# A decoder layer on one core: 8-word and 4-word runs behind the heads, the last output units, and the gate's transpositions inside two other blocks of a head

## The chip, the cores and the metric

The kernel runs on one core of a Trainium2 chip. Its engines are named as the profile names them: PE (TensorE matmul), PEld (its weight loads), DVE (VectorE), ACT (ScalarE), POOL (GpSimd) and SP (SyncE, which only issues transfers here). The metric is the time of one execution in device microseconds; of several runs the median counts.

## The reference

The reference is a decoder trunk of depth one: attention, the residual, and a final norm. All is float32, with 256 positions and a width of 4096.

```python
proj = rms_norm(x, norm_attn) @ w_in            # 256 x 4096  @  4096 x 16384 -> q | k | v | gate
z = q @ k.T / sqrt(128)                         # per head, 32 heads of 128, strictly causal
log_fail = where(causal, log_sigmoid(-z), 0)
suffix = cumsum(log_fail, reverse=True) - log_fail
a = where(causal, exp(log_sigmoid(z) + suffix), 0)
o = a @ v                                       # stick-breaking attention
h = x + (o * silu(gate)) @ w_out                # 4096 x 4096
out = rms_norm(h, final_norm)
```

## The kernel before, in words

**Products.** Every float32 operand of the two large multiplications is split into a high and a low fp32r part (`wh`, `wl` of the weights, which stream through PE; `sh`, `sl` of the input's rows and `oh`, `ol` of the gated heads, which are PE's stationary operands). One product of 128 x 128 by 128 x 512 is a triple of matmuls into one accumulator: high by high, high by low, low by high (`mm3`, called by `product`). A triple's matmuls visit their 512 columns in runs of 8 words ("e") or of 4 words ("c"): in the program's order these read `128x4x16x8` and `128x4x32x4`. The results are the same. Which form a matmul has is set by `BEHIND_OTHERS` for the first seven triples behind any other PE work (three letters, one for each matmul of a triple), by `IN_STEP` for the first triple of a step, and is "e" elsewhere. The counter `since_others` starts again with each block of other work, which comes through `ten`.

**Units and steps.** The work is 20 units one behind the other, each in 16 steps over the 4096 rows of the weights. Units 0 to 15 multiply `w_in`, each giving q, k, v and gate of two heads. Units 16 to 19 multiply `w_out`, each giving two blocks of 512 output columns for both halves of the rows. Units 0 and 16 are plain, with 8 triples a step. In the others a step is done in 8 triples ("eight") or, Strassen-like, in 7 ("seven"). A seven-step costs DVE three extra sums of weight tiles (`raw<-raw,raw` and `raw<-raw` in the profile) and POOL an accumulating transfer. The lists `SEVEN` (input units) and `SEVEN_OUT` (output units) say which steps are sevens. Unit 19, the last, takes its steps in the order `LAST_STEPS`, and three of its steps of `SEVEN_OUT` (11, 13, 14) are done as eights.

**Heads.** The two heads of an input unit are worked between the triples of the next unit, as blocks of PE work with ACT and DVE between them: four transpositions of q and k (`tr`), the scores (`z`), the scan of the sums along a row (`scan`: four matmuls into `z`), the transposition of the gate's two tiles (`gated_with`, its own block), and values (`out_of_head`). A ring named "att" holds a single PSUM bank for all these, one block at a time. The gate is made by `gate`: ACT and DVE turn it into its SiLU in place, in `gv_sb`.

**The planner.** Class `Plan` runs the whole program once as a simulation of the engines with costs in nanoseconds, and writes each engine's instructions in the order in which the simulation starts them. Rings (`take` and `give`) stand for buffers, and a work item carries a key: the smaller key goes first on its engine. So a change of a key, a cost or a ring changes the order of many later instructions. On the chip each engine runs its instructions in that order.

**The end.** While an output unit runs, the blocks of the unit before it are finished: DVE adds the residual (`h<-h,xres`), ACT sums the squares (`sq<-h`), DVE multiplies by the final gain (`gain_on`, `h<-h,grow`). Behind the last unit `last_h`, `block_done`, `part_done`, `finish` and `rows_out` finish the last two blocks, make the factor of each row and multiply and store all rows. Rows 128 to 255 are done ahead of rows 0 to 127; names such as `h6_1` are the block and the half of the rows. Keys and the cost of `squares` decide which of these small instructions go first.

Of the kernel before, what the change touches and what calls it, by code (L numbers as in the profile page):

```python
# [19 lines left out]
P = 128  # L20
S = 256
# [15 lines left out]
BEHIND_OTHERS = ("ccc", "ecc", "eee", "cce", "eee", "eee", "ecc")  # L37
# [9 lines left out]
SEVEN_OUT = (1, 2, 4, 5, 7, 10, 11, 13, 14)  # L47
# [17 lines left out]
H_LATER = 6  # L65
ON_SCALAR = ((1, 3, 5), (1, 3))
# [45 lines left out]
class Plan:  # L112
# [72 lines left out]
    def take(self, *names):  # L185
# [12 lines left out]

        return request
# [48 lines left out]
def kernel(  # L248
# [546 lines left out]
    def gate(u):  # L795
# [3 lines left out]
        yield nc.take("gh")  # L799
# [23 lines left out]
    def head(u, i):  # L823
        yield nc.take("att", "gh")
# [14 lines left out]
        yield nc.take("att")  # L839
        z = att.tile([P, BW], F32, tag="att", name=f"z{u}_{i}")  # L840
# [10 lines left out]
        yield nc.take("gh")  # L851
# [13 lines left out]
        yield nc.take("gh", "gh")  # L865
# [14 lines left out]
        yield nc.take("gh")  # L880
# [11 lines left out]
        o = st["both", u, i][:, 1, :]  # L892
# [11 lines left out]
        gated = st["gated", u, i]  # L904
# [3 lines left out]
    def gated_with(u, i):  # L908
        yield nc.until(("gate", u))
        yield nc.take("att")  # L910
        both = st["both", u, i] = att.tile([P, 2, S], F32, tag="att", name=f"o{u}_{i}")
        gT = both[:, 0, :]

        def turn():
            for t in range(NT):
                nc.tensor.transpose(gT[:, t * P : (t + 1) * P], st["gv", u][:, t, i * P : (i + 1) * P], ident)

        yield ten(turn, P, P)
        if i == 0:
            yield nc.take("gh")  # L920
            st["o", u] = wp.tile([P, 4, P], F32, tag="gh", name=f"gated{u}", bufs=ROWS)
        gated = st["gated", u, i] = st["o", u][:, 2 * i : 2 * i + 2, :].rearrange("p a b -> p (a b)")
        yield act(lambda: nc.scalar.copy(gated, gT), S)
        nc.tell(("gated", u, i))
# [113 lines left out]
    def squares(c, t, place, cut, key=None):  # L1038
# [6 lines left out]
            cut.stop - cut.start, key and key - 1e3,  # L1045
# [9 lines left out]
    def block_out(c, t, key):  # L1055
# [10 lines left out]
        yield from gain_on(c, t, key)  # L1066
# [270 lines left out]
```

## Time and profile before

| what | value |
|---|---|
| three runs | 1705.84, 1709.23 and 1709.48 us, median 1709.23 |
| the profiled execution's own time | 1706.34 us |
| its span, from first to last instruction | 1704.6 us |
| PE busy | 1685.6 us (99%), 7776 matmuls |
| DVE busy | 1607.4 us (94%) |
| ACT busy | 1202.5 us (71%) |
| POOL busy | 325.0 us (19%) |

The profiled execution is 2.9 us below the median of the three runs, which lie in two places 3.4 us apart. Matmuls overlap by design in the profile's model: one that is shown as 0.39 us long is followed by the next after 0.22 us, so the distance between starts is what to read, not the duration. Times on the axis count from the start of the span. All lines of the kernel are shown as L131, a helper through which every instruction goes; so the groups are told apart by the names of their tiles.

### The profile page before, as it was taken

To read this page: it belongs to the slowest core of one execution; us is meant where nothing else is said; L and a number is where in the kernel's file an instruction comes from. 1 tells how busy PE (TensorE), PEld (TensorE's weight loads), DVE (VectorE), ACT (ScalarE), POOL (GpSimd) and SP (SyncE) were. 2 spreads that over 40 slices of the span, in tenths; PEclk is the share of its full clock that TensorE was granted. 3 is DMA by queue.
4 is the path that set the end of the run, shared out by engine and by line. 5 is a ranking of instruction groups with operands and counts; after the bars stand their busy time and mean duration, and the time that the engine had idled before them with its cause. 6 is when DMAs were issued, how large, how long until landed. Compare 5 with 4: busy or idle time off the path is not lost.

```text
span 1704.6 us, 25109 instructions
## 1 busy us (share of the span) xinstructions
PE 1685.6 (99%) x7776; PEld 1415.9 (83%) x7776; DVE 1607.4 (94%) x2025; ACT 1202.5 (71%) x1633; POOL 325.0 (19%) x400
## 2 busy tenths in 40 slices
PE   9999999999999999999999999999999999999996
PEld 7888888888888888888888888888888888888785
DVE  8889999999999999999999999999999977999997
ACT  8986767676767676767676768686767765666664
POOL 0012222222222222221212121212122112122110
PEclk9999999999999999999999999999999999999998
DMA  9968887979797878797978797878788977889795
GB/s 348 329 197 246 231 245 220 255 212 256 208 269 196 269 197 272 195 279 195 268 204 261 208 256 213 254 216 248 220 243 224 295 244 241 240 251 284 218 293 187
DMA packets 248439, 412.78 MB, mean 242 GB/s; under 512 B 28016, under 2 KB 72560, under 8 KB 248304
## 3 DMA queue, kind: packets, MB, share of 16 engines
q1 hardware_dynamic: 194544, 354.24, 62.2%
q0 software_dynamic: 53472, 56.65, 20.5%
q8 instruction: 61, 1.00, 0.2%
q14 instruction: 74, 0.61, 0.1%
q10 hardware_dynamic: 288, 0.28, 0.0%
HBM read 402.93 MB, written 8.13 MB: 241 GB/s over the span
## 4 chain that ended last, share of the span: by engine, by line
PE 94%; DVE 3%; issue 1%; DMA 1%; ACT 0%; SPq 0%; DVEq 0%; ACTq 0%
PE acc L131 90%; PE z L131 2%; PE o L131 2%; DVE wl L131 1%; PE tr L131 1%; DVE h L131 0%; DVE raw L131 0%; ACT wh L131 0%; DMA raw<-in_w_in_dram 0%; DMA raw<-in_w_out_dram 0%; DMA xres<-in_x_dram 0%; DVE wh L131 0%; DVE gv_sb L131 0%; SPq L131 0%; DVE scalars L131 0%
## 5 line engine op out<-in xcount | busy, mean ns | idle before, releaser
L131 ACT CAST wh<-raw 128x1024 fp32r<-128x1024 f32 (+1 forms) x989 | 918.2, 969 | 370.8 <-DVE raw L131 166.8
L131 DVE TENSOR_TENSOR wl<-raw,wh 128x1024 fp32r<-128x1024 f32 (+1 forms) x815 | 974.9, 1219 | 56.4 <-ACT wh L131 25.1
L131 PE MATMUL acc<-wh,sh 128*128 128x512 f32 x2048 | 774.3, 390 | 0.3 <-DVE sh L131 0.3
L131 PE MATMUL acc<-wh,sl 128*128 128x512 f32 x1898 | 727.9, 383 | 1.2 <-DVE sl L131 1.2
L131 PE MATMUL acc<-wl,sh 128*128 128x512 f32 x1748 | 669.0, 383 | 0.2 <-DVE wl L131 0.2
L131 POOL DMA_DIRECT2D raw<-in_w_in_dram x300 | 258.6, 957 | 1026.7 <-DMA raw<-in_w_in_dram 424.2
L131 PEld LDWEIGHTS acc<-wh,sh 128*128 128x128 f32 x2048 | 384.1, 188 | 78.0 <-PE acc L131 4.8
L131 PEld LDWEIGHTS acc<-wh,sl 128*128 128x128 f32 x1898 | 355.8, 187 | 67.2 <-DVE sl L131 1.8
L131 PEld LDWEIGHTS acc<-wl,sh 128*128 128x128 f32 x1748 | 328.3, 188 | 54.8 <-DVE wl L131 0.5
L131 DVE TENSOR_TENSOR raw<-raw,raw 128x512 f32<-128x512 f32 x348 | 237.5, 686 | 6.0 <-DMA raw<-in_w_out_dram 2.1
L131 PE MATMUL acc<-wh,oh 128*128 128x512 f32 x512 | 192.6, 384 | 0.6 <-DVE gv_sb L131 0.6
L131 PE MATMUL acc<-wh,ol 128*128 128x512 f32 x488 | 186.7, 383 | 0.0
L131 PE MATMUL acc<-wl,oh 128*128 128x512 f32 x464 | 177.7, 383 | 2.6 <-DVE wl L131 2.6
L131 DVE TENSOR_TENSOR wh<-raw,wh 128x512 fp32r<-128x512 f32 x174 | 119.3, 686 | 1.6 <-ACT wh L131 1.5
L131 DVE TENSOR_TENSOR raw<-raw 128x512 f32<-128x512 f32 x174 | 119.0, 684 | 0.0
L131 PEld LDWEIGHTS acc<-wh,oh 128*128 128x128 f32 x512 | 95.9, 187 | 18.0 <-DVE gv_sb L131 0.9
L131 PEld LDWEIGHTS acc<-wh,ol 128*128 128x128 f32 x488 | 91.5, 187 | 16.4
L131 PEld LDWEIGHTS acc<-wl,oh 128*128 128x128 f32 x464 | 87.0, 187 | 19.3 <-DVE wl L131 3.8
L131 POOL DMA_DIRECT2D raw<-in_w_out_dram x48 | 41.5, 968 | 181.4 <-DMA raw<-in_w_out_dram 78.7
L131 ACT ACTIVATE f<-f 128x384 f32<-128x384 f32 x96 | 50.5, 526 | 3.0
L131 POOL DMA_DIRECT2D p<-spill x27 | 17.5, 692 | 86.5 <-DVE ol L131 44.1
L131 DVE SCALAR_TENSOR_TENSOR gv_sb<-acc,scalars,gv_sb 128x512 f32<-128x512 f32 x45 | 33.5, 744 | 0.0
(83 smaller groups left out, 755.4 us busy)
## 6 DMA issues: line engine op xcount, KB each, us to landing
raw<-in_w_in_dram SPq DMA_DIRECT2D x1024, 256.0 KB, 4.3
raw<-in_w_out_dram SPq DMA_DIRECT2D x256, 256.0 KB, 4.5
raw<-in_w_in_dram POOLq DMA_DIRECT2D x300, 128.0 KB, 5.1
p<-spill POOLq DMA_DIRECT2D x27, 256.0 KB, 4.5
raw<-in_w_out_dram POOLq DMA_DIRECT2D x48, 128.0 KB, 5.1
xr<-in_x_dram SPq DMA_DIRECT2D x16, 256.0 KB, 5.5
xres<-in_x_dram SPq DMA_DIRECT2D x16, 256.0 KB, 6.2
out_dram<-h SPq DMA_DIRECT2D x16, 256.0 KB, 2.8
```

The source lines that it names most:

```text
L131: return self.tc.keep_in_program_order(getattr(self.engine, name)(*args, **kw))
```

## The change

1. **Runs of words.** `BEHIND_OTHERS` keeps 4-word runs in triples one, two and seven behind other work. Triple four now has "eee", and triple seven "cce" where it had "ecc".
2. **Steps of the output units.** In `SEVEN_OUT` step 8 takes the place of step 4. In units 17 and 18 the adjacent sevens were 1,2 and 4,5 and 10,11 and 13,14, with 7 alone. Now they are 1,2 and 7,8 and 10,11 and 13,14, with 5 alone. In the last unit's order the sevens were at places 1, 3, 4, 6, 8 and 12 (counted from 0); now they are at 1, 3, 6, 8, 10 and 12.
3. **The gain.** The key of the gain's multiplication in `block_out` is 8 us later (`GAIN_LATER`).
4. **Rings.** The heads and the gate take the rings "att" and "gh" with `sooner`: they stand ahead of all others that wait for a place.
5. **The gate's transpositions.** `gated_with` is gone. The first tile of the gate is transposed as the fifth matmul of the scan's block, into the last quarter of the scores' bank; the second as the third matmul of the values' block. Each is copied by ACT on its own (128x128), where one copy of 128x256 was made. The first head's scan waits until the gate is made.
6. **A cost.** `squares` costs the planner an instruction more, for reading the accumulator.

```diff
-BEHIND_OTHERS = ("ccc", "ecc", "eee", "cce", "eee", "eee", "ecc")
+BEHIND_OTHERS = ("ccc", "ecc", "eee", "eee", "eee", "eee", "cce")
-SEVEN_OUT = (1, 2, 4, 5, 7, 10, 11, 13, 14)
+SEVEN_OUT = (1, 2, 5, 7, 8, 10, 11, 13, 14)
+GAIN_LATER = 8.0
...
-                ring[2].append(lambda: request(go, k + 1))
+                ring[2].insert(0 if sooner else len(ring[2]), lambda: request(go, k + 1))
...
-        yield nc.take("att")
-        z = att.tile([P, BW], F32, tag="att", name=f"z{u}_{i}")
+        yield nc.take("att", sooner=True)
+        bank = att.tile([P, W], F32, tag="att", name=f"z{u}_{i}")
+        z, gT = bank[:, 0:BW], bank[:, BW:W]
+
+        def turned(to, t):
+            nc.tensor.transpose(to, st["gv", u][:, t, i * P : (i + 1) * P], ident)
...
+        if i == 0:
+            yield nc.until(("gate", u))
...
-        yield ten(scan, BW, BW, P, P)
+            turned(gT, 0)
+
+        yield ten(scan, BW, BW, P, P, P)
...
+        yield act(lambda: nc.scalar.copy(gated[:, 0:P], gT), P)
         nc.give("att")
-        nc.start(gated_with(u, i))
-        yield nc.until(("gated", u, i))
...
-        yield ten(out_of_head, *FULL_P, *FULL_S)
+            turned(gT2, 1)
+
+        yield ten(out_of_head, *FULL_P, *FULL_S, P)
...
+        yield act(lambda: nc.scalar.copy(gated[:, P:S], gT2), P)
...
-            cut.stop - cut.start, key and key - 1e3,
+            (cut.stop - cut.start, 64), key and key - 1e3,
...
-        yield from gain_on(c, t, key)
+        yield from gain_on(c, t, key + GAIN_LATER * 1e3)
```

How this moves instructions is shown at three places. Matrix multiplications of the program before and after are equal in number (7648 beside the warm-up), blocks of other work on PE are 128 where they were 160, and matmuls in 4-word runs 1221 where they were 1515. ACT has 32 instructions more.

**PE, the first head of unit 4, worked in unit 5.** In the names, `acc5_4` is unit 5's fourth accumulator, `wh249` and `wl249` the high and low part of a weight tile, `sh2` and `sl2` the stationary parts of step 2. Before, from the block with the gate's two transpositions to the block with the values:

```order
L131 MATMUL acc5_6_4398<-wh249_4333,sl2_90 128x4x16x8
L131 MATMUL o4_0_4461<-ident_129,gv_sb4_4218 128x128 x2
L131 MATMUL acc5_4_4312<-wh249_4333,sh2_89 128x4x32x4
L131 MATMUL acc5_4_4312<-wl249_4414,sh2_89 128x4x32x4
L131 MATMUL acc5_4_4312<-wh249_4333,sl2_90 128x4x32x4
L131 MATMUL acc5_2_4299<-wh250_4371,sh3_92 128x4x16x8
L131 MATMUL acc5_2_4299<-wl250_4435,sh3_92 128x4x32x4
L131 MATMUL acc5_2_4299<-wh250_4371,sl3_93 128x4x32x4
L131 MATMUL acc5_2_4299<-wh250_4371,sh3_92 128x4x16x8
L131 MATMUL acc5_2_4299<-wl250_4435,sh3_92 128x4x16x8
L131 MATMUL acc5_2_4299<-wh250_4371,sl3_93 128x4x16x8
L131 MATMUL o4_0_4461<-a4_0_4433,gv_sb4_4218 128x256
```

On the same engine after the change, from the end of the scan to the triple behind it:

```order
L132 MATMUL acc5_2_4307<-wh250_4379,sl3_93 128x4x32x4
L132 MATMUL z4_0_4347<-fh4_0_4395,neg_tri_141 128x384
L132 MATMUL z4_0_4347<-fl4_0_4396,neg_tri_141 128x384
L132 MATMUL z4_0_4347<-fh4_0_4395,neg_tri_141 128x128
L132 MATMUL z4_0_4347<-fl4_0_4396,neg_tri_141 128x128
L132 MATMUL z4_0_4347<-ident_129,gv_sb4_4226 128x128
L132 MATMUL acc5_2_4307<-wh250_4379,sh3_92 128x4x32x4
```

The block of its own is gone, and one transposition stands behind the scan's four matmuls; the other stands behind the values in the same manner. The scan itself stands two triples later than the gate's block stood before.

**ACT, the end of the program.** `sq6_1` are the squares of the rows 128 to 255 of block 6, `sq6_0` those of the rows 0 to 127; the first `scalars` behind them is the root of the rows 128 to 255. Before:

```order
L131 ACTIVATE sq6_1_0_16144,squares_of_rows_142<-h6_1_15518 128x256
L131 ACTIVATE sq6_1_256_16149,squares_of_rows_142<-h6_1_15518 128x256
L131 ACTIVATE sq6_0_0_16159,squares_of_rows_142<-h6_0_15517 128x512
L131 ACTIVATE scalars_77<-squares_of_rows_142,scalars_77 128x1
L131 ACTIVATE scalars_77<-scalars_77 128x1
L131 ACTIVATE h1_1_13963<-h1_1_13963,scalars_77 128x512
```

After:

```order
L132 ACTIVATE sq6_1_0_16174,squares_of_rows_142<-h6_1_15547 128x256
L132 ACTIVATE sq6_1_256_16181,squares_of_rows_142<-h6_1_15547 128x256
L132 ACTIVATE scalars_77<-squares_of_rows_142,scalars_77 128x1
L132 ACTIVATE scalars_77<-scalars_77 128x1
L132 ACTIVATE sq6_0_0_16193,squares_of_rows_142<-h6_0_15546 128x512
L132 ACTIVATE h1_1_13995<-h1_1_13995,scalars_77 128x512
```

The root of the rows 128 to 255 no longer stands behind the squares of the other rows. On DVE the addition `h6_0<-acc19_2,h6_0` has likewise gone from ahead of that root's input to behind it.

**DVE, unit 18, the sevens at steps 10 and 11.** `wl926` to `wl928` belong to step 10, `wl930` is the low part of step 11 for which PE stands before. Before:

```order
L131 TENSOR_TENSOR wl928_15183<-raw299_0_15074,wh928_15168 128x1024
L131 TENSOR_TENSOR h3_14670<-h3_14670,xres3_1_15130 128x512
L131 TENSOR_TENSOR h3_14670<-h3_14670,grow3_15034 128x512
L131 TENSOR_TENSOR wh935_15208<-raw301_1_15097,wh935_15208 128x512
L131 TENSOR_TENSOR raw299_0_15074<-raw299_0_15074,raw299_1_15064 128x2x256
```

After:

```order
L132 TENSOR_TENSOR h3_14706<-h3_14706,xres3_1_15127 128x512
L132 TENSOR_TENSOR raw298_0_15074<-raw298_0_15074 128x2x256
L132 TENSOR_TENSOR wl928_15204<-raw299_0_15138,wh928_15195 128x1024
L132 TENSOR_TENSOR wl926_15213<-raw298_1_14993,wh926_15162 128x1024
L132 TENSOR_TENSOR wl927_15220<-raw298_0_15074,wh927_15176 128x1024
L132 TENSOR_TENSOR raw299_0_15138<-raw299_0_15138,raw299_1_15082 128x2x256
L132 TENSOR_TENSOR wh935_15237<-raw301_1_15165,wh935_15237 128x512
L132 TENSOR_TENSOR raw299_1_15082<-raw299_0_15138,raw299_1_15082 128x2x256
L132 TENSOR_TENSOR h3_14706<-h3_14706,grow3_15027 128x512
```

The gain's multiplication followed its addition at once; now seven other instructions stand between the two.

More of the change, by code (lines that the diff above doesn't have):

```diff
@@ L183, in ring, with take @@
         self.rings[name] = [places, 0, []]
-    def take(self, *names):
+    def take(self, *names, sooner=False):
         def request(go, k=0):
@@ L798, in gate @@
         n = NT * CW
-        yield nc.take("gh")
+        yield nc.take("gh", sooner=True)
         l = wp.tile([P, NT, CW], F32, tag="gh", name=f"gl{u}", bufs=ROWS)
@@ L823, in head @@
     def head(u, i):
-        yield nc.take("att", "gh")
+        yield nc.take("att", "gh", sooner=True)
         tr = att.tile([P, 2, S], F32, tag="att", name=f"tr{u}_{i}")
@@ L850, in head @@
         nc.give("gh")
-        yield nc.take("gh")
+        yield nc.take("gh", sooner=True)
         f = wp.tile([P, BW], F32, tag="gh", name=f"f{u}_{i}", bufs=ROWS)
@@ L876, in scan @@
             nc.tensor.matmul(z[:, 2 * P : BW], neg_one, fl[:, 0:P], stop=True, **kw)
-        yield ten(scan, BW, BW, P, P)
+            turned(gT, 0)
+        yield ten(scan, BW, BW, P, P, P)
         nc.give("gh", "gh")
-        yield nc.take("gh")
+        if i == 0:
+            yield nc.take("gh", sooner=True)
+            st["o", u] = wp.tile([P, 4, P], F32, tag="gh", name=f"gated{u}", bufs=ROWS)
+        gated = st["o", u][:, 2 * i : 2 * i + 2, :].rearrange("p a b -> p (a b)")
+        yield nc.take("gh", sooner=True)
         a = wp.tile([P, BW], F32, tag="gh", name=f"a{u}_{i}", bufs=ROWS)
@@ L888, in head @@
         yield act(weights_of, (BW, BW))
+        yield act(lambda: nc.scalar.copy(gated[:, 0:P], gT), P)
         nc.give("att")
-        nc.start(gated_with(u, i))
-        yield nc.until(("gated", u, i))
-        o = st["both", u, i][:, 1, :]
+        yield nc.take("att", sooner=True)
+        bank2 = att.tile([P, BW], F32, tag="att", name=f"o{u}_{i}")
+        o, gT2 = bank2[:, 0:S], bank2[:, S:BW]
         v = lambda t: st["gv", u][:, t, CW + i * P : CW + (i + 1) * P]
@@ L903, in head @@
             nc.give("two")
-        gated = st["gated", u, i]
+        yield act(lambda: nc.scalar.copy(gated[:, P:S], gT2), P)
         yield dve(lambda: nc.vector.tensor_tensor(out=gated, in0=o, in1=gated, op=ALU.mult), S)
         nc.give("att")
[L908 to L924, printed above, removed]
     spill = {}
```

2 lines of the change are left out of this document (1 added, 1 removed).

## The prediction, made before the change was run

> **What bounds the kernel now.** I read the page first: the engines' busy time and the chain that ended last. Then I read busy time by stretches, and the waits of PE and of its weight loads.
>
> ```profile
> PE 1685.6 (99%) x7776; PEld 1415.9 (83%) x7776; DVE 1607.4 (94%) x2025; ACT 1202.5 (71%) x1633; POOL 325.0 (19%) x400
> PE 94%; DVE 3%; issue 1%; DMA 1%; ACT 0%; SPq 0%; DVEq 0%; ACTq 0%
> ```
>
> PE is the bound: 99% busy, and 94% of the chain. ACT is idle for 29% of the span. DVE, at 94%, is near to being a second bound. The stretches show where it becomes one. The columns are the window, its length, then busy us and instructions of PE, PEld, DVE, ACT and POOL, PE's granted clock, the share of DMA and GB/s.
>
> ```profile
> ...
> 110.00:1358.00 1248.00, 1248.00 (x5800) 1049.74 (x5799) 1205.18 (x1438) 897.52 (x1167) 263.46 (x313) 1.00 0.84 236
> ...
> 1443.00:1524.00 81.00, 81.00 (x369) 68.89 (x368) 76.79 (x98) 52.04 (x67) 13.83 (x16) 1.00 0.83 243
> 1524.00:1605.00 81.00, 78.68 (x355) 66.00 (x353) 77.31 (x93) 48.58 (x62) 16.64 (x20) 1.00 0.89 261
> 1605.00:1691.00 86.00, 85.75 (x389) 72.60 (x388) 77.02 (x105) 49.35 (x70) 9.19 (x11) 1.00 0.70 222
> ```
>
> The clock is full throughout. In the input units PE is never idle, so there the time is the sum of PE's instructions, and only fewer or shorter ones help. In unit 18 (about 1524 to 1605) PE loses 2.32 us, and in the last unit 0.25; there DVE ends last. Behind 1691 comes the tail of DVE, ACT and stores.
>
> **The gate's transpositions.** The timeline of PE and then of PEld around one block of before (start, duration, instruction); the order beside it is that of unit 4's first head:
>
> ```profile
> 445.99 0.39 PE L131 MATMUL acc<-wh,sl 128*128 128x512 f32 x1
> 446.22 0.38 PE L131 MATMUL o<-ident,gv_sb 128*128 128x128 f32 x2
> 446.36 0.47 PE L131 MATMUL acc<-wh,sh 128*128 128x512 f32 x1
> 446.67 0.39 PE L131 MATMUL acc<-wl,sh 128*128 128x512 f32 x1
> 446.89 0.38 PE L131 MATMUL acc<-wh,sl 128*128 128x512 f32 x1
> 447.11 0.39 PE L131 MATMUL acc<-wh,sh 128*128 128x512 f32 x1
> 447.34 0.39 PE L131 MATMUL acc<-wl,sh 128*128 128x512 f32 x1
> 447.58 0.39 PE L131 MATMUL acc<-wh,sl 128*128 128x512 f32 x1
> 447.81 0.39 PE L131 MATMUL acc<-wh,sh 128*128 128x512 f32 x1
> ...
> 448.26 0.39 PE L131 MATMUL acc<-wh,sl 128*128 128x512 f32 x1
> ```
>
> Undisturbed starts stand 0.22 to 0.24 apart. From 445.99 to 446.67 there are two intervals, 0.45 without the block, and 0.68 are taken: 0.23 for it. From 445.99 to 448.26 there are nine in 2.27 us; at 0.22 they are 1.98, which leaves 0.29. I take the middle, 0.26, times 32 blocks (16 units of two heads): 8.3 us leave PE.
>
> They come back as a third or fifth matmul of other blocks. What one costs there, before doesn't show. The nearest rows are the end of the scan's block, where narrow matmuls follow each other:
>
> ```profile
> 442.58 0.22 PE L131 MATMUL z<-fh,neg_tri 128*128 128x128 f32 x1
> 442.64 0.27 PE L131 MATMUL z<-fl,neg_tri 128*128 128x128 f32 x1
> ...
> 442.40 0.19 PEld L131 LDWEIGHTS z<-fh,neg_tri 128*128 128x128 f32 x1
> 442.58 0.19 PEld L131 LDWEIGHTS z<-fl,neg_tri 128*128 128x128 f32 x1
> 442.69 0.19 PEld L131 LDWEIGHTS acc<-wh,sh 128*128 128x128 f32 x1
> 442.80 0.19 PEld L131 LDWEIGHTS acc<-wl,sh 128*128 128x128 f32 x1
> ```
>
> The two matmuls start 0.06 apart, but the loads, one for each, start 0.11 apart (442.58, 442.69, 442.80). A transposition brings its own load, so I take 0.11, times 64: 7.0 us. The gain is 8.3 - 7.0 = 1.3. Ends: at 0.06 each they cost 3.8 and the gain is 4.5. At 0.18 (the load of 442.58 behind that of 442.40, where the matmuls still have 384 columns, as an upper end) they cost 11.5, and 3.2 us are lost.
>
> [...]
>
> ACT makes two copies where it made one:
>
> ```profile
> L131 ACT COPY gated<-o 128x256 f32<-128x256 f32 x32 | 11.8, 368 | 18.8 <-PE o L131 18.8
> ```
>
> Were each of the two as long as the one, that is 0.37 x 32 = 11.8 us more of ACT, hidden in its 29% idle; with that cover gone `wh` would be late by as much. The heads end five triples (some 3.3 us) later in their unit. Their banks and rows aren't wanted before the next unit's heads, dozens of triples later; POOL's spill moves with them and is read in unit 16. The instructions of DVE, POOL and SP are the same in number. The new wait on the gate stands ahead of the scan, with all later products queued behind it on PE; it is a rival below. The order at the units' boundaries is unchanged, so what PE loses there stays.
>
> **Words.** Compare in the rows above what follows a 4-word matmul (446.67, 446.89, 447.34, 447.58: intervals 0.22, 0.22, 0.24, 0.23, mean 0.2275) with what follows an 8-word one (447.11: 0.23; 447.81 to 448.26: two intervals of 0.225; mean 0.2267). There are 294 fewer 4-word matmuls. At the 0.001 us of these means that is 0.3 us, at the 0.01 of the rows' resolution 2.9. I take 0.8, nearer to the lower end, since the means show next to nothing.
>
> [...]
>
> **The last units.** The three places where PE waits for DVE's `wl`, each with the matmul ahead of it, then DVE ahead of the largest; in brackets the idle time and what ended it.
>
> ```profile
> 1554.85 0.40 PE L131 MATMUL acc<-wh,oh 128*128 128x512 f32 x1
> 1555.49 0.50 PE L131 MATMUL acc<-wl,oh 128*128 128x512 f32 x1 [0.24 <-DVE wl L131]
> ...
> 1585.26 0.40 PE L131 MATMUL acc<-wh,oh 128*128 128x512 f32 x1
> 1587.74 0.49 PE L131 MATMUL acc<-wl,oh 128*128 128x512 f32 x1 [2.08 <-DVE wl L131]
> ...
> 1632.12 0.39 PE L131 MATMUL acc<-wh,oh 128*128 128x512 f32 x1
> 1632.77 0.48 PE L131 MATMUL acc<-wl,oh 128*128 128x512 f32 x1 [0.26 <-DVE wl L131]
> ...
> 1570.78 0.69 DVE L131 TENSOR_TENSOR h<-h,grow 128x512 f32<-128x512 f32 x1 [0.79 <-ACT sq L131]
> ...
> 1581.05 0.69 DVE L131 TENSOR_TENSOR h<-h,grow 128x512 f32<-128x512 f32 x1 [0.85 <-ACT sq L131]
> ```
>
> With 0.22 taken off each distance the stalls are 0.42, 2.26 and 0.43 us: 3.1. Laid beside the program's order they are steps 5, 11 of unit 18 and step 4 of the last unit, each time the second of two adjacent sevens, whose low part DVE delivers late. Ahead of the largest, DVE itself stood 0.79 + 0.85 = 1.64 us for ACT's squares, because the gain follows its addition at once.
>
> After the change the pair 4,5 is gone, and in the last unit no two sevens are adjacent: 0.42 + 0.43 = 0.85 saved. With the gain later DVE's 1.64 fall away, and 2.26 becomes 0.6. That is 2.5. Against it stands the new pair 7,8, one eight-step ahead of 10,11. In unit 17, which lost nothing before (81.00 of 81.00), I charge the smallest stall seen, 0.4; in unit 18 the mean of the three, 1.0. Net gain 1.1. Ends: 3.1 if all stalls go, and a loss of 2.0 if 7,8 costs 2.26 in both units (2.5 - 4.5). What is late next is DVE's `wl` again, at 95% of both windows.
>
> **The tail.** ACT and DVE in the chain, PE's last matmul:
>
> ```profile
> 1687.31 0.39 ACT L131 ACTIVATE sq<-h 128x256 f32<-128x256 f32 x1
> ...
> 1687.72 0.69 DVE L131 TENSOR_TENSOR h<-acc,h 128x512 f32<-128x512 f32 x1 [0.29 <-PE acc L131]
> 1688.33 0.15 DVE L131 SCALAR_TENSOR_TENSOR scalars<-squares_of_rows,scalars 128x1 f32<-128x1 f32 x1
> ...
> 1688.51 0.60 ACT L131 ACTIVATE sq<-h 128x512 f32<-128x512 f32 x1 [0.69 <-DVE scalars L131]
> 1689.14 0.28 ACT L131 ACTIVATE scalars<-squares_of_rows,scalars 128x1 f32<-128x1 f32 x1
> ...
> 1690.43 1.68 DVE L131 TENSOR_SCALAR h<-h,scalars 128x512 f32<-128x512 f32 x4
> ...
> 1691.26 0.40 PE L131 MATMUL acc<-wh,ol 128*128 128x512 f32 x1
> ...
> 1692.68 0.42 DVE L131 TENSOR_TENSOR h<-acc,h 128x256 f32<-128x256 f32 x1
> ```
>
> The squares of 1687.31 are the last input of the upper rows' factor. Its join on DVE (1688.33) stands behind an addition for other rows (1687.72), and the root on ACT (1689.14) behind that block's squares (1688.51). Both now stand behind. The root can then start near 1688.1, and the row multiplications at 1690.43 start some 1.0 earlier. So does the addition at 1692.68, which needs PE's last accumulator, but that isn't there before 1691.26 + 0.40 = 1691.66. The gain is at most 1.02; I take 0.9. The lower end is 0.4: only the DVE part (1688.33 back to about 1687.9), if the lower rows' moved squares hold up DVE in turn.
>
> **The sum.** 1.3 + 0.8 + 1.1 + 0.9 = 4.1 us less. Against its own execution that is 1706.3 - 4.1 = 1702.2. The runs' median is 2.9 above that execution, so against it the forecast is 1709.2 - 4.1 = 1705.1. The runs of before scatter by 3.6 us; 0.2%, or 3.4 us, is about what a measurement of this kernel can tell from no change.
>
> **Rivals.**
> - *No change to be told* (within 3.4 us). The transpositions cost 0.13 where they go, as much as their block, and the last units' stalls only move: 0.8 + 0.9 and little else, 1707.5. The price 0.11 against 0.13 speaks for it; the two intervals of 0.23 and 0.29 do not settle it.
> - *Slower, by the gate.* The row of the gate's last multiplication on DVE in unit 5 (its start twice):
>
> ```profile
> L131 DVE TENSOR_TENSOR gv_sb<-gv_sb,gl x1: 685/685/685, 445.1 to 445.1; 128x512 f32<-128x512 f32 x1
> ```
>
> It ends at 445.8, and the block that needs it stood at 446.22: a room of 0.4 us. Now the scan waits for it, two triples (1.3 us) later by the order, so the room is some 1.7 us. Where ACT's and DVE's other work brings the gate later than that, PE stands with all products behind it. From 4.1 / 16 = 0.26 us in each unit the change is slower than before; at 0.6, 9.6 us in all, the time is 1709.2 - 4.1 + 9.6 = 1714.7. Against it: the gate's own block was waited for on PE in the same way, with less room, and no stall showed there.
> - *More.* Each transposition costs 0.06 (3.2 more), all the last stalls go (2.0 more): 1709.2 - 9.3 = 1699.9. For it speaks that PE's matmuls there start 0.06 apart; against it that the loads do not.
> - *Words are dear*: runs of 4 cost their upper end, 2.9 instead of 0.8, and the time is 1703.0, inside the forecast's side. Against it stand the two means above. [...]
>
> **Chances.** The forecast, with its own range of 1702 to 1707: 0.46, of which 0.04 within 0.2%, since its sum stands only 0.7 us from that bound. *More*: 0.14. *Words are dear*: 0.04. No change to be told: 0.24. Slower by the gate: 0.12, of which 0.02 within 0.2%. So faster 0.42 + 0.14 + 0.04 = 0.60, same 0.04 + 0.24 + 0.02 = 0.30, slower 0.10. The range goes from 1699.9, which leaves out half of *More*, to 1709.4, about where the time stays without any gain, which leaves out the gate: 0.07 + 0.12.
>
> **What would show it.** PE with 7776 matmuls and a busy time some 3 us less; no block `o<-ident` on its own; loads 0.11 apart behind the scan. Stalls of PE for DVE `wl` at step 11 of unit 18 of some 0.6 us, none in the last unit, and one at step 8 of 1 us or less. The first row multiplication of the tail (1690.43 before, 0.8 ahead of PE's last matmul) about 1.8 ahead of it. A wait of PE `z` for DVE `gv_sb` would show the second rival. What would make this wrong is above all an appended transposition that costs 0.18, or stalls at 7,8.

## The result, and the profile after

The changed kernel takes 1698.68 us (median of five, 1697.83 to 1699.30) against 1709.23 (five, 1705.84 to 1710.10): a ratio of 0.9942, with a 95% interval of 0.9929 to 0.9955. It is faster by 10.5 us, where 4.1 were forecast, and it lies 1.2 us below the range. The two profiled executions, 1706.34 and 1698.90 us, differ by 7.4 us only. So there are two questions: where the 7.4 us come from, and where the other 3 do.

The page of the changed kernel, its first part and the chain that ended last:

```profile
PE 1680.2 (99%) x7776; PEld 1417.4 (84%) x7776; DVE 1602.0 (94%) x2025; ACT 1206.7 (71%) x1665; POOL 324.9 (19%) x400
...
PE 94%; DVE 3%; DMA 1%; issue 1%; ACT 1%; SPq 0%; DVEq 0%; ACTq 0%
```

PE bounds the kernel as before. It has as many matmuls, and ACT has the 32 copies more. Busy time by stretches, with the columns of the prediction, shows that the output units lose less:

```profile
110.00:1354.00 1244.00, 1243.91 (x5800) 1051.05 (x5800) 1200.85 (x1438) 903.24 (x1198) 263.18 (x313) 1.00 0.83 237
...
1438.00:1519.00 81.00, 80.71 (x366) 68.20 (x366) 76.94 (x96) 50.46 (x65) 14.02 (x17) 1.00 0.82 245
1519.00:1600.00 81.00, 79.92 (x363) 67.67 (x362) 77.85 (x93) 50.40 (x64) 16.51 (x20) 1.00 0.86 256
1600.00:1685.00 85.00, 84.84 (x384) 71.50 (x382) 78.28 (x109) 49.86 (x71) 9.22 (x11) 1.00 0.75 231
```

The same 5800 matmuls of the input units now need 4 us less. Unit 18 loses 1.08 us instead of 2.32, unit 17 loses 0.29 instead of nothing. The two places on PE, each with the matmul ahead of it:

```profile
1514.92 0.39 PE L132 MATMUL acc<-wh,oh 128*128 128x512 f32 x1
1515.60 0.50 PE L132 MATMUL acc<-wl,oh 128*128 128x512 f32 x1 [0.29 <-DVE wl L132]
...
1579.87 0.40 PE L132 MATMUL acc<-wh,oh 128*128 128x512 f32 x1
1581.34 0.49 PE L132 MATMUL acc<-wl,oh 128*128 128x512 f32 x1 [1.08 <-DVE wl L132]
```

Less 0.22 each, the stalls are 0.46 and 1.25 us, where there were 0.42, 2.26 and 0.43. The large one is again at step 11 of unit 18. The tail, from the timelines of ACT, DVE and PE:

```profile
1680.44 0.39 ACT L132 ACTIVATE sq<-h 128x256 f32<-128x256 f32 x1
1680.99 0.29 ACT L132 ACTIVATE scalars<-squares_of_rows,scalars 128x1 f32<-128x1 f32 x1
1681.63 0.60 ACT L132 ACTIVATE sq<-h 128x512 f32<-128x512 f32 x1
...
1680.68 0.16 DVE L132 SCALAR_TENSOR_TENSOR scalars<-squares_of_rows,scalars 128x1 f32<-128x1 f32 x1
1684.93 0.42 DVE L132 TENSOR_TENSOR h<-acc,h 128x256 f32<-128x256 f32 x1
...
1684.44 0.40 PE L132 MATMUL acc<-wh,ol 128*128 128x512 f32 x1
```

The root follows its squares after 0.55 us (1680.44 to 1680.99), where it was 1.83. The addition of 1684.93 comes 0.49 behind the start of PE's last matmul, where it was 1.42; it has reached that matmul's end (1684.44 + 0.40 = 1684.84).

I split the distance from PE's first product to its last, 1685.2 us before and 1678.7 after, by what stands between the starts of consecutive matmuls:

| part of PE's time | after less before |
|---|---|
| blocks of other work, each from the product ahead of it to the second one behind it (less 0.44 for the two intervals between products) | -2.0 us |
| one wait of PE for DVE early in unit 16 | -0.8 us |
| what the regular intervals between products (up to 260 ns) exceed 220 ns, summed (11.5 us before, 8.5 after) | -3.0 us |
| all other stalls (the first unit +0.6, the other input units +0.2, the output units -1.5) | -0.7 us |
| sum | -6.5 us |

The place of the second row, before and after:

```profile
1362.33 0.27 PE L131 MATMUL z<-off,ident_b 128*128 128x256 bf16 x1
1363.17 0.49 PE L131 MATMUL acc<-wh,oh 128*128 128x512 f32 x1 [0.56 <-DVE gv_sb L131]
...
1357.68 0.27 PE L132 MATMUL z<-off,ident_b 128*128 128x256 bf16 x1
1357.70 0.47 PE L132 MATMUL acc<-wh,oh 128*128 128x512 f32 x1
```

This wait costs 0.8 to 1.8 us in every profile in which the gate has its own block, and it stands in none in which its transpositions are moved.

From PE's last matmul to the end of the span it is 13.3 us before and 12.7 after: 0.7 less. The rest, 0.3 us, lies ahead of PE's first product. The third row is the surprise: the forecast had 0.8 for it.

### The profile page after: what moved, and what is told of

Its sections match the earlier page's. It is cut to its first block, busy times and chain, and to the rows that moved or that the text cites. A ratio compares the mean times of both kernels' runs of the same rounds, so it can differ in the third digit from the quotient of the medians.

```text
span 1697.1 us, 25128 instructions
## 1 busy us (share of the span) xinstructions
PE 1680.2 (99%) x7776; PEld 1417.4 (84%) x7776; DVE 1602.0 (94%) x2025; ACT 1206.7 (71%) x1665; POOL 324.9 (19%) x400
## 4 chain that ended last, share of the span: by engine, by line
PE 94%; DVE 3%; DMA 1%; issue 1%; ACT 1%; SPq 0%; DVEq 0%; ACTq 0%
PE acc L132 89%; PE z L132 3%; PE o L132 1%; DVE wl L132 1%; PE tr L132 1%; DVE h L132 1%; DVE raw L132 0%; ACT wh L132 0%; DMA raw<-in_w_out_dram 0%; DMA raw<-in_w_in_dram 0%; DMA xres<-in_x_dram 0%; SPq L132 0%; ACT sq L132 0%; DVE scalars L132 0%; DVE qk_sb L132 0%
```

## The experiments

Ratios are to the kernel before, timed on the same chip beside each kernel; their intervals are some 0.001 either way, 1.7 us. Where two changed kernels are compared, it is by their medians; their ratios say the same within some 1.5 us. No run has the rings' rule (point 4) without the moved transpositions, and none has the squares' cost (point 6) alone.

### The parts alone

Words alone:

```diff
-BEHIND_OTHERS = ("ccc", "ecc", "eee", "cce", "eee", "eee", "ecc")
+BEHIND_OTHERS = ("ccc", "ecc", "eee", "eee", "eee", "eee", "cce")
```

> Only the runs of words are changed: triple four eee, triple seven cce. The order of all engines is that of before. As predicted: 0.8 us less, not to be told from no change. What the trace after suggests instead (an interval from a 4-word matmul to an 8-word one is 0.226, other intervals 0.220): some 1.5 to 3 us less. If the scatter of before stays with this kernel, the words have nothing to do with it.

Measured: 1705.45 against 1708.13 us, ratio 0.9986 (0.9978 to 0.9995): 2.4 us. The excess over 220 ns is 9.3 us in its profile; the two profiles of before have 11.5 and 10.7. The forecast's 0.8 was too small by a factor of three, though the interval (0.9 to 3.8 us) nearly reaches it, and 2.4 lies within the ends of 0.3 and 2.9 that the forecast gave this term.

The gate's transpositions alone:

```diff
+            turned(gT, 0)
...
+            turned(gT2, 1)
...
-        nc.start(gated_with(u, i))
```

> Only the gate's transpositions are moved into the scan's and the values' blocks, with the rings' new rule; words, output steps, gain and the squares' cost are those of before. As predicted: 1.3 us less. What the trace after gives for it (0.25 us for each block that is gone, 0.09 for each transposition that comes back): 8.0 - 5.7 = 2.3 us less. The stalls of the output units should be as before; if they differ, the planner has moved more than the heads.

Measured: 1708.48 against 1708.13 us, ratio 1.0003 (0.9993 to 1.0012): nothing. Yet the blocks in its profile are shorter by 1.7 us, and the wait in unit 16 is gone, 2.5 us in all. They are given back: the excess over 220 ns is 14.9 us, 3.4 more than before.

The end alone:

```diff
-SEVEN_OUT = (1, 2, 4, 5, 7, 10, 11, 13, 14)
+SEVEN_OUT = (1, 2, 5, 7, 8, 10, 11, 13, 14)
...
-        yield from gain_on(c, t, key)
+        yield from gain_on(c, t, key + 8.0 * 1e3)
...
-            cut.stop - cut.start, key and key - 1e3,
+            (cut.stop - cut.start, 64), key and key - 1e3,
```

> Only the end is changed: step 8 for step 4 in the output units, the gain 8 us later, the squares' cost. As predicted: 1.1 + 0.9 = 2.0 us less. By theory A, in which the executions of before lose a varying time in unit 18, the median falls by 4 to 5 us and the scatter of the executions shrinks to the 1.5 us that the changed kernel shows; by rival B the median falls by about 2 and the scatter stays at 4.

Measured: 1703.96 against 1708.13 us, ratio 0.9972 (0.9962 to 0.9983), with executions from 1703.0 to 1705.3 where those of before beside it went from 1705.2 to 1711.2. That is 4.2 to 4.8 us, more than twice the 2.0 of the forecast, and much of the scatter has gone with it, as theory A said. The distance from PE's last matmul to the end is 1.0 of it (12.4 against 13.3 us).

The three parts add up to some 7 us, not to 10. So two things were open: what words and gate do to each other, and why a stall costs more than its length.

### Words and gate on each other

The changed kernel with the old words:

```diff
-BEHIND_OTHERS = ("ccc", "ecc", "eee", "eee", "eee", "eee", "cce")
+BEHIND_OTHERS = ("ccc", "ecc", "eee", "cce", "eee", "eee", "ecc")
```

> The changed kernel with the old runs of words (triple four cce, triple seven ecc again). If the parts add up (words alone were 2.4 us, the gate alone nothing): about 2.4 us slower than the changed kernel, 1701. If words and the gate's blocks work on each other: in the profile of the gate alone the products behind the heads run at about 224 ns for some 40 matmuls instead of falling to 220 after 9, and the new words end that; then this kernel loses 5 to 6 us against the changed one, 1704, nothing of the gate's part is left, and the interval between products stays above 222 ns in many more places than in the changed kernel.

Measured: 1704.71 us, ratio 0.9983 (0.9974 to 0.9992), 6.0 us above the changed kernel; the excess over 220 ns is 14.6 us against 8.5. The parts don't add up: the same edit of the words is worth 2.4 us beside the old blocks and 6 beside the new ones.

Words and gate together, with the old end:

```diff
-BEHIND_OTHERS = ("ccc", "ecc", "eee", "cce", "eee", "eee", "ecc")
+BEHIND_OTHERS = ("ccc", "ecc", "eee", "eee", "eee", "eee", "cce")
...
+            turned(gT, 0)
...
+            turned(gT2, 1)
...
-        nc.start(gated_with(u, i))
```

> Before, with the new words and the gate's transpositions moved, and the old end. If the parts add up: 2.4 us less than before. If they work on each other: 5 to 6 us less, 1702.5. By the theory on the clock (a stall of 2.25 us in unit 18 makes the chip grant half the clock for some microseconds behind it in most executions), the executions still scatter over 4 us or more, since the stall is still there.

Measured: 1701.06 against 1707.76 us, ratio 0.9964 (0.9952 to 0.9977): 6.1 to 6.7 us. The excess is 8.2 us. Its five executions scattered by 1.7 us only, although its stall in unit 18 is still 2.4 us long; here the theory on the clock was not borne out, with few executions.

Three kernels more ask what the words do, by the pattern behind other work:

```diff
-BEHIND_OTHERS = ("ccc", "ecc", "eee", "eee", "eee", "eee", "cce")
+BEHIND_OTHERS = ("eee",) * 7
```

> The changed kernel with 8-word runs in all seven triples behind other work; the steps' own pattern stays. If each change from 4-word to 8-word runs costs some 6 to 10 ns and nothing else (as the mean intervals suggested): about 300 fewer changes, 2 to 3 us faster, 1696. If the 4-word runs right behind a block are what brings the products back to 220 ns: slower, by some ns on tens of products behind each of 128 blocks, 3 to 10 us, 1702 to 1709, with the interval above 222 ns for longer behind each block.

Measured: 1711.00 us, ratio 1.0017 (1.0008 to 1.0026): 12.3 us slower than the changed kernel, more than was expected. The timeline of PE behind the second head's values in unit 5, first for the changed kernel and then with 8-word runs only; between the first and the last row of each stand 36 intervals:

```profile
470.05 0.47 PE L132 MATMUL acc<-wh,sh 128*128 128x512 f32 x1
470.36 0.38 PE L132 MATMUL acc<-wl,sh 128*128 128x512 f32 x1
...
471.48 0.39 PE L132 MATMUL acc<-wh,sh 128*128 128x512 f32 x1
471.70 0.38 PE L132 MATMUL acc<-wl,sh 128*128 128x512 f32 x1
...
479.40 0.38 PE L132 MATMUL acc<-wh,sh 128*128 128x512 f32 x1
```

```profile
474.08 0.47 PE L132 MATMUL acc<-wh,sh 128*128 128x512 f32 x1
474.39 0.39 PE L132 MATMUL acc<-wl,sh 128*128 128x512 f32 x1
...
475.52 0.40 PE L132 MATMUL acc<-wh,sh 128*128 128x512 f32 x1
475.76 0.39 PE L132 MATMUL acc<-wl,sh 128*128 128x512 f32 x1
...
483.83 0.39 PE L132 MATMUL acc<-wh,sh 128*128 128x512 f32 x1
```

From 471.48 to 479.40 they take 7.92 us, 0.220 each. From 475.52 to 483.83 they take 8.31, 0.231 each. No engine is waited for in either, the granted clock is 1.00 in both (469 to 480 us and 471 to 484), and the products between are of the same kinds. What differs is what stood in the six matmuls ahead (three 4-word ones, then an 8-word one and two of 4 words; or six of 8 words) and two 4-word matmuls in triple seven, which the last kernel of this section does without. So here the words right behind a block decide how fast the products behind them run, 0.220 or 0.231 us each, for 36 intervals.

```diff
-BEHIND_OTHERS = ("ccc", "ecc", "eee", "eee", "eee", "eee", "cce")
+BEHIND_OTHERS = ("ccc",) * 7
```

> The changed kernel with 4-word runs in all seven triples behind other work. If changes of form cost and forms don't: fewer changes, 1 us faster, 1697.5. If a 4-word product is itself slower behind a block, or the last change, which now comes in triple eight, upsets the products again: slower, 2 to 6 us, 1701 to 1705. The mean interval at each place behind a block says which.

Measured: 1706.22 us, ratio 0.9989 (0.9980 to 0.9998), 7.5 us slower than the changed kernel, a little more than was expected, with an excess of 16.3 us. 4-word runs in all seven triples are better than none (1711.00), but lose more than half of what those in the first two give.

```diff
-BEHIND_OTHERS = ("ccc", "ecc", "eee", "eee", "eee", "eee", "cce")
+BEHIND_OTHERS = ("ccc", "ecc", "eee", "eee", "eee", "eee", "eee")
```

> The changed kernel with 8-word runs in triple seven too, so that 4-word runs stand in triples one and two alone. If what counts is the first two triples, which bring the products back to 220 ns by the tenth: 0.5 to 1 us faster, 1698, since the last change of form behind each block goes too. If triple seven does something for those blocks that don't settle by then: slower by 1 to 3 us, and the excess over 220 ns at places 10 to 30 behind a block (1.0 us in all in the changed kernel) rises.

Measured: 1698.26 us, ratio 0.9946 (0.9933 to 0.9960): as fast as the changed kernel (1698.68). The excess falls from 8.5 to 7.9 us, so the 4-word runs of triple seven aren't needed; triples one and two do it.

The excess over 220 ns, by the place of a product behind the last block (in matmuls; intervals over 260 ns, the stalls, are left out):

| kernel | all | places 2 to 9 | 10 to 30 | 31 to 98 | later |
|---|---|---|---|---|---|
| before | 11.5 us | 6.7 | 3.2 | 0.3 | 1.2 |
| words alone | 9.3 | 6.9 | 0.9 | 0.5 | 1.1 |
| gate alone | 14.9 | 5.1 | 4.9 | 3.4 | 1.5 |
| changed, old words | 14.6 | 4.8 | 5.0 | 3.4 | 1.4 |
| words and gate | 8.2 | 5.9 | 1.0 | 0.3 | 1.0 |
| changed | 8.5 | 5.7 | 1.0 | 0.2 | 1.5 |
| 8-word runs in all seven triples | 22.4 | 7.9 | 9.7 | 3.3 | 1.6 |
| 4-word runs in all seven | 16.3 | 5.3 | 7.3 | 2.3 | 1.4 |
| 4-word runs in triples one and two | 7.9 | 5.7 | 0.5 | 0.3 | 1.4 |

Five more profiles show how far such a sum scatters. With the words and blocks of before, the second profile of before, the end alone, the step list alone and the gain alone have 10.7, 12.1, 10.3 and 11.6 us in all; with those of the changed kernel, the changed kernel with the gain where it was has 8.2.

The first ten places cost 5 to 8 us everywhere. The kernels differ more in whether the products are back at 220 ns after that. In the old pattern the 4-word runs of triple four (places 10 and 11) stand just where the products have settled, and upset them again: places 10 to 30 cost 3.2 us with them and 0.9 without beside the old blocks (before, words alone), 5.0 and 1.0 beside the new ones (changed, old words; changed). Beside the old blocks the products recover in some 20 places (0.3 us at places 31 to 98), beside the new ones not for some 40 (3.4 us).

### What a stall costs beside its length

The kernel before once more, without an edit:

> The kernel before once more, as a second profile and to see how its executions scatter. The two profiles at hand differ by 7.5 us of span, the medians by 10.5. Theory A (the 3 us between are single executions of before that lose more in unit 18): this one's executions lie between 1705 and 1710 again, and a profile above 1708 shows the stall of PE for DVE wl in units 17 and 18 larger than the 3.1 us of the first profile. Rival B (the 3 us lie elsewhere, in the first unit's loads or at the end's stores): the stalls in units 17 and 18 are 3.1 us as before, and the distance from the last matmul to the end, or the start, differs.

Measured: 11 executions from 1706.39 to 1711.61, median 1708.47, ratio 1.0003. The profiled one, 1706.88 us, shows what the first profile of before doesn't. By stretches, first this one and then the first profile, behind the stall at step 11 of unit 18:

```profile
1585.00:1588.00 3.00, 1.32 (x6) 1.12 (x7) 3.00 (x4) 1.23 (x2) 0.00 (x0) 1.00 1.05 314
1588.00:1590.00 2.00, 2.00 (x7) 1.51 (x6) 2.00 (x3) 0.00 (x0) 0.00 (x0) 0.51 1.05 378
1590.00:1592.00 2.00, 2.00 (x7) 1.62 (x6) 1.39 (x3) 1.02 (x2) 0.00 (x0) 0.63 0.91 344
1592.00:1594.00 2.00, 2.00 (x10) 1.69 (x9) 1.94 (x2) 1.22 (x3) 0.00 (x0) 1.00 0.06 23
```

```profile
1588.00:1590.00 2.00, 2.00 (x10) 1.62 (x10) 2.00 (x3) 0.00 (x0) 0.00 (x0) 1.00 1.03 354
1590.00:1592.00 2.00, 2.00 (x11) 1.62 (x10) 1.97 (x4) 0.00 (x0) 0.00 (x0) 1.00 1.03 371
```

PE is granted 0.51 and 0.63 of its clock for some 3 us, soon after the stall ends, and does 14 matmuls in 4 us where the other execution does 21. That costs 1.6 us. In the first profile of before the same stall of 2.25 us stands, and no half clock follows (1.00 in both stretches). So not every such stall is followed by it. And the half clock behind this stall isn't all that the slower executions lose: the execution that shows it took 1706.88 us, 1.6 less than the median of the eleven.

So the changed kernel was given a longer stall: at step 11 of unit 18 DVE makes the low part that PE waits for once more, or twice more.

```diff
+        more_once = 1 if n == 930 else 0        # 2 in the second kernel
+
+        def low():
+            for _ in range(1 + more_once):
+                minus(l, full, h)
...
-        yield dve(lambda: minus(l, full, h), size, key, more=10)
+        yield dve(low, size, key, more=10)
```

> The changed kernel, in which DVE makes the low part that PE waits for at step 11 of unit 18 twice (1.15 us more, same result). The stall there is 1.25 us in the changed kernel, so 2.4 here: the size it had before. If a stall costs its own length alone: 1.2 us slower than the changed kernel, some 1699.9, executions within 2 us of each other, and a mean granted clock of 0.9978 as there. By the theory on the clock: 1.2 us and some 1.5 to 2 us on top in most executions, median 1701 to 1702, a scatter of 4 us, and a mean clock of about 0.9967, as all kernels with a stall of 2.2 us or more have shown.

Measured: 1700.42 us, with single executions at 1699.8, 1700.4, 1700.4, 1702.5 and 1704.0 and clocks of 0.998, 0.997, 0.998, 0.997 and 0.996. The stall has grown by 1.4 us, to 2.65. The cost is 1.7 us in the median, or 3.1 by the ratios; three executions paid about the stall's length, two paid 4 and 5. "Most executions" was wrong, "some" is right. The profiled one is the 1704.0; PE's timeline there:

```profile
1582.21 0.40 PE L132 MATMUL acc<-wh,oh 128*128 128x512 f32 x1
1585.08 0.79 PE L132 MATMUL acc<-wl,oh 128*128 128x512 f32 x1 [2.47 <-DVE wl L132]
1585.67 0.63 PE L132 MATMUL acc<-wh,ol 128*128 128x512 f32 x1
1586.10 0.63 PE L132 MATMUL acc<-wh,oh 128*128 128x512 f32 x1
1586.52 0.63 PE L132 MATMUL acc<-wl,oh 128*128 128x512 f32 x1
...
1588.22 0.38 PE L132 MATMUL acc<-wh,ol 128*128 128x512 f32 x1
```

The products stand 0.43 apart behind the stall (granted 0.50 from 1586 to 1588 us), and 0.22 again from 1588.22 on. This execution also lost 2.4 us at the first unit's loads and 1.7 us at half clock behind them, so its 1704.0 isn't the step's alone.

> As the last, with the low part made three times: a stall of some 3.5 us. By length alone: 2.3 us slower than the changed kernel, 1701.0, clock 0.9978. By the theory on the clock: the half clock now comes in nearly every execution, 4 to 5 us slower, 1703 to 1704, clock 0.996 or lower, and the profile shows intervals of 0.43 us behind the stall.

Measured: 1702.54 us (six executions, 1700.28 to 1705.08), 3.9 above the changed kernel (4.4 by the ratios) for 2.3 us of stall more, with a mean clock of 0.9968. Between the two theories, and nearer to that on the clock. All kernels by the longest stall in their profile's output units:

| kernel | longest stall | executions | median | their spread | mean clock |
|---|---|---|---|---|---|
| changed, gain where it was | 0.5 us | 5 | 1696.5 us | 1.3 us | 0.9974 |
| changed, 8-word runs in all seven triples | 0.8 | 11 | 1711.0 | 5.5 | 0.9975 |
| changed, old words | 0.9 | 11 | 1704.7 | 2.0 | 0.9975 |
| end alone | 1.1 | 8 | 1704.0 | 2.3 | 0.9975 |
| changed | 1.3 | 5 | 1698.7 | 1.5 | 0.9978 |
| changed, 4-word runs in all seven | 1.4 | 11 | 1706.2 | 3.5 | 0.9975 |
| changed, 4-word runs in triples one and two | 1.4 | 5 | 1698.3 | 1.1 | 0.9976 |
| gain alone | 1.4 | 11 | 1705.0 | 2.9 | 0.9976 |
| step list alone | 1.8 (unit 16; 0.6 behind it) | 9 | 1702.6 | 2.7 | 0.9979 |
| before (beside all others) | 2.3 | 88 | 1707.9 | 6.0 | 0.9967 |
| words alone | 2.3 | 11 | 1705.5 | 3.8 | 0.9969 |
| gate alone | 2.3 | 12 | 1708.5 | 8.1 | 0.9966 |
| words and gate | 2.4 | 5 | 1701.1 | 1.7 | 0.9968 |
| low part twice | 2.7 | 5 | 1700.4 | 4.2 | 0.9972 |
| low part three times | 3.6 | 6 | 1702.5 | 4.8 | 0.9968 |

Stalls up to 1.8 us go with a mean clock of 0.9974 or more, stalls from 2.3 us with 0.9972 or less; the step between the two is small, as each execution's clock is given to 0.001 only. A difference of 0.001 is 1.7 us of 1705. The spread follows the stall less well: with 8-word runs alone it is 5.5 us. In the profiles half clock follows the stall in 4 of the 7 with a stall of 2.2 us or more (before, in one of two; gate alone; low part twice and three times), and in none of the 9 others. Within the 88 executions of before those at a clock of 0.998 took 1706.0 us in the mean, at 0.997 1707.6, at 0.996 1709.0 and at 0.995 1710.0. The profile at hand for the forecast was one of the quick ones.

Half clock isn't bound to that stall. In the first unit the gain alone has 3.3 us of it, soon after a wait of 1.42 us:

```profile
6.86 0.46 PE L131 MATMUL acc<-wh,sh 128*128 128x512 f32 x1 [1.42 <-ACT wh L131]
...
8.60 0.63 PE L131 MATMUL acc<-wl,sh 128*128 128x512 f32 x1
9.03 0.63 PE L131 MATMUL acc<-wh,sl 128*128 128x512 f32 x1
```

The first products of words and gate, and of the step list alone, also stand 0.43 apart up to 10.6 us. In these three it costs next to nothing, as the first unit waits for its data in any case (2.3 to 2.5 us lost, 1.8 to 2.8 in profiles without it), but an execution's mean clock may count it too. It counts the end as well: behind PE's last matmul the first profile of before shows 0.56 from 1695 to 1700 us and 0.50 from there to its end at 1704.6, that of the changed kernel 0.50 from 1689 us to its end at 1697.1. So the mean clock alone doesn't say where an execution lost its time.

### Which part of the end took the stall away

The step list alone:

```diff
-SEVEN_OUT = (1, 2, 4, 5, 7, 10, 11, 13, 14)
+SEVEN_OUT = (1, 2, 5, 7, 8, 10, 11, 13, 14)
```

> Only step 8 for step 4 in the output units. As predicted for this piece: the last unit's stall (0.43) and that at the pair 4,5 (0.42) go, the pair 7,8 adds up to 1.4: no change within 1 us. The stall of 2.25 us at step 11 of unit 18 should stay, as the gain still stands at its addition; then the scatter of 4 to 6 us stays too. If the stall shrinks here, the step list made the room and not the gain.

Measured: 1702.58 us, ratio 0.9971 (0.9961 to 0.9981): all that the three edits of the end gave together. The expectation of no change was wrong. Of the stalls for a low part none over 0.6 us is left, although the gain still stands at its addition; the wait early in unit 16 is longer than before, 1.8 us. Its tail is 1.4 us shorter than that of before (11.9 us from PE's last matmul to the end, against 13.3).

The gain alone:

```diff
-        yield from gain_on(c, t, key)
+        yield from gain_on(c, t, key + 8.0 * 1e3)
```

> Only the gain is 8 us later. As predicted for this piece: DVE's 1.64 us of waiting for the squares go, and the stall of 2.25 us at step 11 becomes 0.6; the other two (0.4 each) stay. By the theory on the clock the median falls by 1.6 and by some 2 us more, since the half clock goes with the stall, and the executions lie within 2 us of each other. Without that theory: 1.6 us less, scatter as before.

Measured: 1704.99 us, ratio 0.9985 (0.9977 to 0.9994), spread 2.9 us. At step 11 of unit 18 only 0.1 us is left, but its largest stall now stands at step 5:

```profile
1556.96 0.40 PE L131 MATMUL acc<-wh,oh 128*128 128x512 f32 x1
1558.60 0.49 PE L131 MATMUL acc<-wl,oh 128*128 128x512 f32 x1 [1.24 <-DVE wl L131]
```

In all its output units stall for 4.1 us, where before they stalled for 3.4; yet it is 2.8 us faster. Half of that is the tail, 11.9 us as in the last kernel. The rest, some 1.4 us in spite of 0.7 us more of stalls, speaks for the clock and against the length.

The changed kernel with the gain where it was:

```diff
-        yield from gain_on(c, t, key + GAIN_LATER * 1e3)
+        yield from gain_on(c, t, key)
```

> The changed kernel with the gain straight behind its squares again. If the gain made the room on DVE, as the prediction had it: the stall at step 11 of unit 18 is back at 2.2 us or more, the mean clock falls to 0.9967 and the time to 1700.5 or worse. If the step list made it (step list alone: no stall over 0.6): as fast as the changed kernel or faster, 1697.5 to 1698.7, with stalls of about 0.5 and clock 0.998.

Measured: 1696.53 us, ratio 0.9936 (0.9924 to 0.9948), the fastest of all. It is faster than the changed kernel by 2.2 us, by the ratios by 1.0 only, with intervals that overlap; the kernel with 4-word runs in triples one and two, which has the later gain and was timed beside it on the same chip, is 1.7 us slower. One large stall is left:

```profile
1580.03 0.40 PE L132 MATMUL acc<-wh,oh 128*128 128x512 f32 x1
1580.78 0.49 PE L132 MATMUL acc<-wl,oh 128*128 128x512 f32 x1 [0.36 <-DVE wl L132]
```

So the step list made the room on DVE. Once it is there, the later gain gives nothing and costs 1 to 2 us: its stalls are 1.9 against 0.7 us, and its tail is 12.7 against 11.9.

## Why the prediction was wrong

The direction was right, and the forecast was less than half of the gain.

- **"I take 0.8, nearer to the lower end, since the means show next to nothing."** This step of the part on words failed most. The means compared a 4-word with an 8-word matmul, and that price is small indeed. What the words do is another thing: they decide whether the products behind a block run at 220 or at 225 to 231 ns, for up to some 40 products. Alone they were worth 2.4 us, still within the term's ends, beside the gate's new blocks 6.0, twice its upper end. The row that I used, one stretch of nine matmuls, couldn't show it; the intervals at every place behind all blocks could have.
- **"8.3 - 7.0 = 1.3".** The mechanism was right. In the two profiles the 32 blocks cost 7.6 us, 0.24 each, and the 64 transpositions 5.9: 0.08 each behind the scan and 0.10 behind the values, instead of 0.11. So their own gain is 1.7 us. But the term stood alone, and the parts don't stand alone: with the old words the gate's gain was lost to slower products, and with the new ones it was about 4 us (1705.45 to 1701.06, or 0.9986 to 0.9964).
- **"The order at the units' boundaries is unchanged, so what PE loses there stays."** It didn't: the wait of 0.8 us early in unit 16 went with the moved transpositions. The sum had nothing for it.
- **"With the gain later DVE's 1.64 fall away, and 2.26 becomes 0.6."** It became 1.25. The last unit's stall and that at 4,5 went as said; the pair 7,8 stalls nowhere, but one stall of 0.46 came near the end of unit 17. In the profiles the output units' stalls fell from 3.4 to 1.9 us, 1.5 against the 1.1 of the forecast. The cause was put wrongly in part: the step list alone does it (0.6 at most left). The later gain alone takes the stall at step 11 away as well, but others grow in its place (4.1 us in all), and beside the step list it is no help.
- **The price of a stall was its length.** This is the step that is missing from the sum. A stall of 2.3 us cost up to 1.6 us of half clock beside (0.51 and 0.63 granted in the second profile of before), in some executions; with 2.3 us added to the stall the kernel lost 1.6 to 2.1 us more than that length. The first profile of before happened to be without it, and its windows, all at 1.00, made it look excluded.
- **"The runs' median is 2.9 above that execution, so against it the forecast is 1709.2 - 4.1".** That took the 2.9 for an offset which the change would leave alone. Between the 88 executions' median of 1707.9 and the profile of 1706.3 lie 1.6 us, and the slower executions have the lower clocks. That this is the half clock behind the stall is argued, from the medians and clocks with and without the stall; only two executions of before were profiled, and the one with the half clock was 0.5 us longer than the other. What is left of the 10.5, some 1.3 us, is the draw of five executions.
- **The tail, 0.9.** Right: the last rows' factor comes 3.7 us behind the start of PE's last matmul instead of 4.7. What follows the factor gave 0.3 of it back. That the squares' cost did it isn't shown: the step list alone and the gain alone, without it, shorten the tail by 1.4 us.
- **The rivals.** No wait of PE's scan for the gate showed in any kernel with the moved transpositions. *Words are dear* had the right place, at half the size and with the wrong mechanism: were the shorter runs dearer, 8-word runs would be the better ones everywhere; with them in all seven triples the kernel was slowest (1711.00 us). *More*, at 1699.9, came nearest to the time, for other reasons.

## What to carry to other kernels

PE, the bound engine and 99% busy, still had two modes here, products 0.220 us apart or 0.225 to 0.231: look at the distribution of the intervals between equal instructions, by their place behind a disturbance, before an edit is priced by a mean. Edits that touch the same engine's rhythm are tried together as well as apart; here one part was worth nothing or 4 us, by the other. And where executions scatter, ask what the granted clock was in each: a kernel with one stall of 2.3 us was slower than one with several of at most 1.4 and more in sum, by some 1.4 us more than its longer tail explains.

## What the runs showed of the hardware

- Equal products of 512 columns ran 0.220 us apart or, behind blocks of narrow work, 0.225 (4-word runs in all seven triples) to 0.231 (8-word runs in all seven) apart for dozens of products. Which of the two depended on the runs of words in the first triples behind the block. A first triple in 4-word runs and a second with one 8-word and two 4-word matmuls, with 8-word runs behind them, brought the products to 0.220 by the fourth triple (0.5 us of excess at places 10 to 30); the same two with 4-word runs again in triple four (changed, old words: 5.0 us), 8-word runs alone (9.7), or 4-word runs for seven triples (7.3), didn't. Why was not found: the profile shows no wait and no lower clock (1.00 with 0.220 and with 0.231).
- Gaps of 2.1 to 2.5 us without work on PE, amid a stream of products, were followed by half clock (0.50 to 0.63 granted, products 0.43 apart) of some 3 us in some executions and not in others: 2.1 us in the second profile of before and in the gate alone, but not in the first profile of before or with the words alone. In the first unit a gap of 1.4 us, with shorter ones behind it, was once followed by it too. What decides is open.
